# Moving one column in sixteen from VectorE to ScalarE in a streaming variance kernel, with a re-cut tail

## The chip, the cores and the metric

The kernel runs on one core of one Trainium2 chip. The metric is the device time of one execution, in microseconds (us). Engines: ScalarE is ACT, VectorE is DVE, GpSimd is POOL, and SyncE (SP) only issues DMAs here; TensorE does no work.

## The reference

```python
# x: 32 x 512 x 1024, float32
mean_sq = np.mean(x**2, axis=-1)
sq_mean = np.mean(x, axis=-1)**2
return (mean_sq - sq_mean).astype(np.float32)      # 32 x 512
```

It is the variance of each of the 16,384 rows of 1024 numbers. Every row is read once (67.1 MB), and one number a row is written.

## The kernel before

**Columns.** A "column" is 128 rows of 1024 numbers, one row a partition: 128 columns in all, 0.52 MB each. Columns 0 to 95 pass through a loop as six groups of 16, through two buffers `xt[0]` and `xt[1]` of 16 columns. Columns 96 to 127 are the tail, with loads of its own that get smaller: 8, 8, 5, 4, 2, 2, 1 and 1 columns (`END_LOADS`, L51), and the last column in two halves (`PIECES`, L55). The first 16 tail columns land in `xt[0]`, the others in `xt_end`.

**Two ways to a variance.** DVE takes a column with two `bn_stats` of 512 numbers each (L118, or L244 and L248 in the tail, L260 for the last column) and one `bn_aggr` that joins the two halves (L225 in the loop, L253 and L267 in the tail). ACT takes a column with two passes over its 1024 numbers: L122 sums to the negated mean, L127 squares with that mean as bias and sums to the variance. Each ACT pass is followed by an instruction that reads the accumulator. ACT makes several means and then as many variances: a "batch" of three columns in the loop (`ACT_BATCH`).

**A group in the loop.** DVE waits for the landing (L215) and gives ACT the word to begin (`go`, L216). ACT has the first 6 columns of the 16 (`NACT`, L49), DVE the other 10: twenty `bn_stats`, then ten `bn_aggr`. Ahead of the last of these, DVE waits until ACT has finished its 6 columns (`act_done`, L224); the last `bn_aggr` then raises `done` (L226). SP waits on `done` before it loads the next group into the freed buffer (L157, L158); the tail's loads wait for the fifth `done`, which is group 4's (L159), and follow one another on SP (L161 to L169).

**The tail.** `END_WHO` (L52) says who takes which tail column: 11 go to ACT and 20 to DVE, and the last column of all to DVE. DVE can begin the tail only behind the last `bn_aggr` of the last group. For the first 11 of its tail columns (`JOINED`, those in the first two loads) DVE makes the `bn_stats` alone, and POOL joins the halves in nine steps and a last one for each unbroken run of columns (L180 to L209). The other 9, and the last column, DVE joins itself, one column behind.

**Stores.** SP writes columns 0 to 15 early (L306), columns 16 to 120 when POOL, ACT and DVE have passed certain steps (L307 to L310), and the last 7 columns when ACT and DVE are done (L311 to L313).

**Where the code lies.** L146 and L147 place the code of ACT and DVE from slot 128 (`HEAD`) of a block of 256 instruction slots. By the built program, DVE has 128 instructions from that point to the end of the kernel (not counting branches to the very next instruction, which take no time in the trace), and waits that stand by themselves among them.

Of the kernel before, what the change touches and what calls it, by code (L numbers as in the profile page):

```python
# [11 lines left out]
def kernel(  # L12
# [15 lines left out]
    P = nc.NUM_PARTITIONS  # L28
    FP32 = mybir.dt.float32
# [5 lines left out]
    N, D = xf.shape  # L35
    assert N % P == 0
    ncols = N // P
# [6 lines left out]
    GROUP = 16  # L44
    NBUF = 2
    TURNS = 3
    PER_TURN = NBUF * GROUP
    END0 = TURNS * PER_TURN
    NACT = 6  # L49
    ACT_BATCH = 3  # L50
    END_LOADS = [8, 8, 5, 4, 2, 2, 1, 1]  # L51
    END_WHO = "AADDDDDD" "AAADDDDD" "AADDD" "AADD" "DD" "AD" "D" "A"  # L52
    FIRST = END_LOADS[0] + END_LOADS[1]
    JOINED = END_WHO[:FIRST].count("D")
    PIECES = [512, 512]  # L55
    EARLY = 4
    HEAD = 128
# [1 line left out]
    def sbuf(name, shape, dtype):  # L59
        return nc.alloc_sbuf_tensor(name, shape, dtype).ap()  # L60

    def psum(name, shape, dtype):
        return nc.alloc_psum_tensor(name, shape, dtype).ap()

    xt = [sbuf(f"xt{b}", [P, GROUP, D], FP32) for b in range(NBUF)]
    xt_end = sbuf("xt_end", [P, ncols - END0 - FIRST, D], FP32)
    mv = sbuf("mv", [P, 2, ncols], FP32)
    stage = sbuf("stage", [P, PER_TURN, 2], FP32)
    stats = sbuf("stats", [P, PER_TURN, 2, 6], FP32)
    stats_join = sbuf("stats_join", [P, JOINED, 2, 6], FP32)  # L70
    stats_end = sbuf("stats_end", [P, ncols - END0, 4, 6], FP32)
    neg_mean = sbuf("neg_mean", [P, PER_TURN], FP32)
    neg_mean_end = sbuf("neg_mean_end", [P, ncols - END0], FP32)
    two = sbuf("two", [P, JOINED, 2], FP32)
    mu = sbuf("mu", [P, JOINED, 1], FP32)
    dev = sbuf("dev", [P, JOINED, 4], FP32)
    junk = [sbuf(f"junk{i}", [P, D], mybir.dt.bfloat16) for i in range(ACT_BATCH)]
    junk_sq = [psum(f"junk_sq{i}", [P, D], FP32) for i in range(ACT_BATCH)]

    sync, act, dve, gps = nc.sync, nc.scalar, nc.vector, nc.gpsimd  # L80
    landed = [nc.alloc_semaphore(f"landed{b}") for b in range(NBUF)]
    NEND = len(END_LOADS) + len(PIECES)
    landed_end = [nc.alloc_semaphore(f"landed_end{b}") for b in range(NEND)]
# [10 lines left out]
    def load(dst, c0, n, sem, f0=0, f=D):  # L94
        b0, pitch, row0 = next(b for b in BLOCKS if b[0] <= c0 < b[0] + b[1])
        assert c0 + n <= b0 + pitch
        ap = [[pitch * D, P], [D, n], [1, f]] if n > 1 else [[pitch * D, P], [1, f]]
        sync.dma_start(  # L98
            out=dst,
            in_=dataclasses.replace(xf, offset=(row0 + c0 - b0) * D + f0, ap=ap),  # L100
        ).then_inc(sem, 16)
# [10 lines left out]
    def take(engine, sem, n):  # L112
        engine.wait_ge(sem, n)
        engine.sem_inc(sem, -n)  # L114
# [6 lines left out]
    def act_mean(i, xcol, nm):  # L121
        return act.activation(  # L122
            out=junk[i], in_=xcol, func=ACTF.Copy, scale=-S / D, accum_out=nm
        )

    def act_var(i, xcol, nm, var):
        return act.activation(  # L127
            out=junk_sq[i], in_=xcol, func=ACTF.Square, scale=S, bias=nm, accum_out=var
        )

    def end_col(c):
        k = c - END0
        return xt[0][:, k, :] if k < FIRST else xt_end[:, k - FIRST, :]

    end_cols = []
    at = END0
    for b, n in enumerate(END_LOADS):
        end_cols += [(b, c, END_WHO[c - END0]) for c in range(at, at + n)]
        at += n
    assert at == ncols - 1 and sum(PIECES) == D  # L140
    early = END0 + sum(END_LOADS[:EARLY])
    act_step_of, dve_step_of = {}, {}
    joined = [c for b, c, who in end_cols if who == "D"][:JOINED]
    assert joined[-1] < END0 + FIRST and TURNS * NBUF >= NBUF + 1

    for engine in (act, dve):  # L146
        engine.addr_align(FETCH_BLOCK_INSTRUCTIONS, offset=HEAD, max_nops=0)  # L147
# [12 lines left out]
    c = END0  # L160
    for b, n in enumerate(END_LOADS):  # L161
        k = c - END0
# [3 lines left out]
    f = 0  # L166
    for b, n in enumerate(PIECES, len(END_LOADS)):
        load(end_col(c)[:, f : f + n], c, 1, landed_end[b], f, n)
        f += n  # L169

    gps.sem_inc(copied, 1)
    for t in range(TURNS):
# [11 lines left out]
        lambda: gps.tensor_scalar(out=mu, in0=mu, scalar1=0.25, scalar2=None, op0=ALU.mult),  # L184
        lambda: gps.tensor_tensor(out=dev, in0=mean, in1=mu.to_broadcast([P, JOINED, 4]), op=ALU.subtract),
        lambda: gps.tensor_tensor(out=dev, in0=dev, in1=dev, op=ALU.mult),
# [25 lines left out]
    with nc.Fori(0, TURNS, engines=[ENG.DVE]):  # L212
        take(dve, copied, 1)
        for b in range(NBUF):
            take(dve, landed[b], 16)  # L215
            dve.sem_inc(go, 1)  # L216
            mine = range(b * GROUP + NACT, (b + 1) * GROUP)
            for j in mine:
# [11 lines left out]
    for b, c, who in end_cols:  # L230
        if who != "D":
            continue
        if b != seen:
            dve.wait_ge(landed_end[b], 16)
            seen = b
        col = end_col(c)
        if c in joined:
            last = halves(stats_join[:, joined.index(c), :, :], col)
            if c == joined[-1]:
                last.then_inc(dve_step, 1)  # L240
                n += 1
            continue
        st = stats_end[:, c - END0, :2, :]
        dve.bn_stats(out=st[:, 0, :], in_=col[:, :H])  # L244
        if waiting:
            waiting()
        n += 1
        dve.bn_stats(out=st[:, 1, :], in_=col[:, H:]).then_inc(dve_step, 1)  # L248
        dve_step_of.setdefault(b, n)

        def waiting(n=n, c=c, st=st):
            dve.wait_ge(dve_step, n)
            return dve.bn_aggr(out=mv[:, :, c], in_=st)  # L253

    c = ncols - 1
    st = stats_end[:, c - END0, : len(PIECES), :]
    f = 0
    for i, size in enumerate(PIECES):
        dve.wait_ge(landed_end[len(END_LOADS) + i], 16)
        last = dve.bn_stats(out=st[:, i, :], in_=end_col(c)[:, f : f + size])  # L260
        if i == 0:
            waiting()
        f += size
# [7 lines left out]
    with nc.Fori(0, TURNS, engines=[ENG.Activation]):  # L271
        for b in range(NBUF):
            take(act, go, 1)
            for i0 in range(0, NACT, ACT_BATCH):
                mine = range(b * GROUP + i0, b * GROUP + i0 + ACT_BATCH)
                for i, j in enumerate(mine):
                    last = act_mean(i, xt[b][:, i0 + i, :], neg_mean[:, j : j + 1])
                last.then_inc(act_step, 1)
                take(act, act_step, 1)
                for i, j in enumerate(mine):  # L280
                    last = act_var(
                        i, xt[b][:, i0 + i, :], neg_mean[:, j : j + 1], stage[:, j, 1:2]
                    )
            last.then_inc(act_done, 1)
    n = 0
    for b in range(len(END_LOADS)):
        mine = [c for bb, c, who in end_cols if bb == b and who == "A"]
# [59 lines left out]
```

## Time and profile before

| | |
|---|---|
| time, median of 3 runs (lowest, highest) | 163.88 us (163.84, 163.90) |
| time of the profiled execution, and its span | 163.92 us, 162.6 us |
| busy: DVE, ACT, POOL | 103.8, 106.3, 3.6 us |
| HBM read, mean rate over the span | 67.11 MB, 413 GB/s |
| share of the DMA engines' span taken by loads and stores | 96.4% |
| `bn_stats` L118 in the loop | 120, mean 677 ns |
| ACT's mean pass L122, and its accumulator read | 41, mean 1043 ns; 186 ns |
| ACT's variance pass L127 in the loop, and its accumulator read | 36, mean 1104 ns; 186 ns |
| DVE's wait for ACT ahead of the last `bn_aggr` of a group | 0.88 us in each of the six |

The span is what the profiler saw of the program itself; the execution is 1.3 us longer. Durations of neighbouring instructions overlap a little (an engine starts the next before the last has quite ended), so that a run of them is reckoned by the distance between starts, which the timeline gives.

### The profile page before, as it was taken

The numbers are of one execution on the slowest core, as the hardware profiler recorded it, in microseconds if no ns is written. First come the engines' busy times: TensorE is split into PE (matmuls) and PEld (weight loads), VectorE is DVE, ScalarE is ACT, GpSimd is POOL, SyncE is SP. The second block draws the span as 40 slices with busy tenths as digits, with TensorE's granted clock in tenths as the row PEclk, the third lists the DMA queues.
The fourth block names the chain that finished last, engine by engine and source line by source line (L and its number), as shares of the span: only waits on it lengthen the run. The fifth ranks groups of instructions, "written<-read, shape, count | busy, mean of one in ns | idle before, by whom it ended". The sixth has DMA issues, their size and how long they took to land. (4 is left out here: it accounts for less than half of the span.)

```text
span 162.6 us, 570 instructions
## 1 busy us (share of the span) xinstructions
DVE 103.8 (64%) x232; ACT 106.3 (65%) x189; POOL 3.6 (2%) x18
## 2 busy tenths in 40 slices
DVE  0000029980599607994099922998049979999994
ACT  3000029990599807995099932999149999799965
POOL 0000000000000000000000000000000000006000
DMA  7969979989998996996996997997989999999990
GB/s 262 516 290 484 516 322 451 516 355 419 516 419 355 516 484 290 516 500 274 516 500 274 516 516 306 468 516 339 435 387 427 468 395 417 448 416 409 414 356 7
DMA packets 2739, 67.20 MB, mean 413 GB/s; under 512 B 688, under 2 KB 688, under 8 KB 1200
## 3 DMA queue, kind: packets, MB, share of 16 engines
q1 hardware_dynamic: 2736, 67.18, 96.4%
q14 instruction: 3, 0.02, 0.1%
HBM read 67.11 MB, written 0.07 MB: 413 GB/s over the span
## 5 line engine op out<-in xcount | busy, mean ns | idle before, releaser
L118 DVE BATCH_NORM_STATS2 stats<-xt 128x6 f32<-128x512 f32 x120 | 71.8, 677 | 50.0 <-DVEq L114 50.0
L122 ACT ACTIVATE junk<-xt 128x1024 bf16<-128x1024 f32 x41 | 42.7, 1043 | 49.1 <-ACTq L114 48.0
L127 ACT ACTIVATE junk_sq<-xt,neg_mean 128x1024 f32<-128x1024 f32 x36 | 39.7, 1104 | 1.5
L118 DVE BATCH_NORM_STATS2 stats_join<-xt 128x6 f32<-128x512 f32 x22 | 13.2, 676 | 0.0
L225 DVE BATCH_NORM_AGGREGATE stage<-stats 128x2 f32<-128x12 f32 x60 | 6.0, 166 | 6.2 <-DVEq L114 5.3
L122 ACT ACTIVATION_READ_ACCUMULATOR junk<-xt 128x1 f32 x41 | 7.6, 186 | 0.0
L122 ACT ACTIVATE junk<-xt_end 128x1024 bf16<-128x1024 f32 x6 | 6.3, 1046 | 1.4 <-DMA xt_end<-in_x_dram 1.4
L127 ACT ACTIVATE junk_sq<-xt_end,neg_mean_end 128x1024 f32<-128x1024 f32 x6 | 6.7, 1110 | 0.1
L127 ACT ACTIVATION_READ_ACCUMULATOR junk_sq<-xt,neg_mean 128x1 f32 x36 | 6.7, 186 | 0.0
L244 DVE BATCH_NORM_STATS2 stats_end<-xt_end 128x6 f32<-128x512 f32 x9 | 6.1, 678 | 0.4 <-DMA xt_end<-in_x_dram 0.4
L248 DVE BATCH_NORM_STATS2 stats_end<-xt_end 128x6 f32<-128x512 f32 x9 | 5.8, 642 | 0.0
L127 ACT ACTIVATE junk_sq<-xt,neg_mean_end 128x1024 f32<-128x1024 f32 x5 | 5.5, 1105 | 0.1
L174 POOL COPY mv<-stage 128x32 f32<-128x32 f32 x3 | 0.6, 209 | 133.2 <-DVE stage L225 133.2
L270 ACT ACT_TABLE_LOAD x1 | 1.3, 1283 | 2.8 <-PEq L154 2.8
L253 DVE BATCH_NORM_AGGREGATE mv<-stats_end 128x2 f32<-128x12 f32 x9 | 1.7, 192 | 0.0
L260 DVE BATCH_NORM_STATS2 stats_end<-xt_end 128x6 f32<-128x512 f32 x2 | 1.3, 669 | 0.5 <-DMA xt_end<-in_x_dram 0.5
L127 ACT ACTIVATION_READ_ACCUMULATOR junk_sq<-xt_end,neg_mean_end 128x1 f32 x6 | 1.1, 187 | 0.0
L122 ACT ACTIVATION_READ_ACCUMULATOR junk<-xt_end 128x1 f32 x6 | 1.1, 186 | 0.0
L127 ACT ACTIVATION_READ_ACCUMULATOR junk_sq<-xt,neg_mean_end 128x1 f32 x5 | 0.9, 187 | 0.0
L182 POOL TENSOR_TENSOR two<-stats_join 128x22 f32<-128x22 f32 x1 | 0.3, 252 | 12.9 <-DVE stats_join L118 12.9
L201 POOL TENSOR_SCALAR mv<-mu 128x6 f32<-128x6 f32 (+1 forms) x2 | 0.5, 237 | 0.2
L187 POOL TENSOR_SCALAR dev<-dev 128x44 f32<-128x44 f32 x1 | 0.3, 332 | 0.1
(12 smaller groups left out, 2.3 us busy)
## 6 DMA issues: line engine op xcount, KB each, us to landing
xt<-in_x_dram SPq DMA_DIRECT2D x2, 4096.0 KB, 19.5
xt_end<-in_x_dram SPq DMA_DIRECT2D x1, 2560.0 KB, 29.8
xt_end<-in_x_dram SPq DMA_DIRECT2D x1, 2048.0 KB, 34.1
xt_end<-in_x_dram SPq DMA_DIRECT2D x2, 1024.0 KB, 37.2
xt_end<-in_x_dram SPq DMA_DIRECT2D x2, 512.0 KB, 40.4
xt_end<-in_x_dram SPq DMA_DIRECT2D x2, 256.0 KB, 40.9
xt<-in_x_dram SPq DMA_DIRECT2D x6, 24.5
out_dram<-mv SPq DMA_DIRECT2D x1, 52.5 KB, 5.3
```

Of the source, the lines that this page charges most:

```text
L118: last = dve.bn_stats(out=st[:, h, :], in_=xcol[:, h * H : (h + 1) * H])
L122: return act.activation(out=junk[i], in_=xcol, func=ACTF.Copy, scale=-S / D, accum_out=nm)
L127: return act.activation(out=junk_sq[i], in_=xcol, func=ACTF.Square, scale=S, bias=nm, accum_out=var)
L174: gps.tensor_copy(out=mv[:, 1, t * PER_TURN : (t + 1) * PER_TURN], in_=stage[:, :, 1]).then_inc(copied, 1)
L182: lambda: gps.tensor_tensor(out=two, in0=mean[:, :, 0:2], in1=mean[:, :, 2:4], op=ALU.add),
L201: lambda j=j, c=c, n=n: gps.tensor_scalar(out=mv[:, 1, c : c + n], in0=mu[:, j : j + n, 0], scalar1=1.0 / D, scalar2=None, op0=ALU.mult,)
L225: last = dve.bn_aggr(out=stage[:, j, :], in_=stats[:, j, :, :])
L244: dve.bn_stats(out=st[:, 0, :], in_=col[:, :H])
L248: dve.bn_stats(out=st[:, 1, :], in_=col[:, H:]).then_inc(dve_step, 1)
L253: return dve.bn_aggr(out=mv[:, :, c], in_=st)
L260: last = dve.bn_stats(out=st[:, i, :], in_=end_col(c)[:, f : f + size])
L270: act.preload_act_table(ACTF.Square)
```

## The change

ACT takes 7 of the 16 columns of a group, in batches of 4 and 3, and DVE 9. Four scratch buffers of ACT in place of three. The tail's loads become 8, 7, 6, 4, 2, 2, 1, 1 and two halves; of its columns ACT takes 10 and DVE 21 and the last. POOL joins 15 of DVE's tail columns in place of 11: those of the first three loads. The last column moves to the slot of `xt[0]` that the shorter second load leaves free. DVE's code in the loop and tail has 7 instructions fewer: a column's three, twice, in the loop, and one in the tail: 121 in place of 128 by the same count.

```diff
-    NACT = 6
-    ACT_BATCH = 3
-    END_LOADS = [8, 8, 5, 4, 2, 2, 1, 1]
-    END_WHO = "AADDDDDD" "AAADDDDD" "AADDD" "AADD" "DD" "AD" "D" "A"
+    NACT = 7
+    ACT_BATCHES = [(0, 4), (4, 7)]
+    END_LOADS = [8, 7, 6, 4, 2, 2, 1, 1]
+    END_WHO = "ADDDDDDD" "AAADDDD" "AADDDD" "AADD" "DD" "AD" "D" "A"
     FIRST = END_LOADS[0] + END_LOADS[1]
-    JOINED = END_WHO[:FIRST].count("D")
+    JOINED = END_WHO[: FIRST + END_LOADS[2]].count("D")
...
-    xt_end = sbuf("xt_end", [P, ncols - END0 - FIRST, D], FP32)
+    xt_end = sbuf("xt_end", [P, ncols - 1 - END0 - FIRST, D], FP32)
...
-    junk = [sbuf(f"junk{i}", [P, D], mybir.dt.bfloat16) for i in range(ACT_BATCH)]
-    junk_sq = [psum(f"junk_sq{i}", [P, D], FP32) for i in range(ACT_BATCH)]
+    junk = [sbuf(f"junk{i}", [P, D], mybir.dt.bfloat16) for i in range(4)]
+    junk_sq = [psum(f"junk_sq{i}", [P, D], FP32) for i in range(4)]
...
     def end_col(c):
         k = c - END0
+        if c == ncols - 1:
+            return xt[0][:, FIRST, :]
         return xt[0][:, k, :] if k < FIRST else xt_end[:, k - FIRST, :]
...
-            for i0 in range(0, NACT, ACT_BATCH):
-                mine = range(b * GROUP + i0, b * GROUP + i0 + ACT_BATCH)
+            for i0, i1 in ACT_BATCHES:
+                mine = range(b * GROUP + i0, b * GROUP + i1)
```

More of the change, by code (lines that the diff above doesn't have):

```diff
@@ L143 @@
     joined = [c for b, c, who in end_cols if who == "D"][:JOINED]
-    assert joined[-1] < END0 + FIRST and TURNS * NBUF >= NBUF + 1
     for engine in (act, dve):
```

## The prediction

> **What bounds the kernel now.** First the page: its DMA line and queues say that loads move through most of the span.
>
> ```profile
> span 162.6 us, 570 instructions
> ...
> DMA  7969979989998996996996997997989999999990
> ...
> q1 hardware_dynamic: 2736, 67.18, 96.4%
> ```
>
> The dips are no pauses: a load moves in packets of 64 KB, and the engines finish them together. Groups begin on DVE every 19.36 us (61.89, 81.25, 100.61, 119.96), and 8.39 MB in 19.36 us is 433 GB/s, all along. So up to the last landing the loads set the pace. Next, what a group costs behind its landing, from the timeline (start, length, engine):
>
> ```profile
> 81.25 11.96 DVE L118 BATCH_NORM_STATS2 stats<-xt 128x6 f32<-128x512 f32 x20 [5.37 <-DVEq L114]
> 93.36 0.79 DVE L225 BATCH_NORM_AGGREGATE stage<-stats 128x2 f32<-128x12 f32 x9
> 95.03 0.21 DVE L225 BATCH_NORM_AGGREGATE stage<-stats 128x2 f32<-128x12 f32 x1 [0.88 <-DVEq L114]
> ```
>
> DVE's last join of the group stands 0.88 us behind the nine others: it waits for ACT. ACT is the longer engine in every group (all six have this row), and 5.4 us of the period are left for both. Third, the last group and the tail on DVE, and the end:
>
> ```profile
> 133.74 0.21 DVE L225 BATCH_NORM_AGGREGATE stage<-stats 128x2 f32<-128x12 f32 x1 [0.88 <-DVEq L114]
> 133.92 13.15 DVE L118 BATCH_NORM_STATS2 stats_join<-xt 128x6 f32<-128x512 f32 x22
> ...
> 146.99 0.68 DVE L244 BATCH_NORM_STATS2 stats_end<-xt_end 128x6 f32<-128x512 f32 x1
> ...
> 157.44 0.69 DVE L244 BATCH_NORM_STATS2 stats_end<-xt_end 128x6 f32<-128x512 f32 x1 [0.38 <-DMA xt_end<-in_x_dram]
> ...
> 159.31 0.69 DVE L260 BATCH_NORM_STATS2 stats_end<-xt_end 128x6 f32<-128x512 f32 x1 [0.51 <-DMA xt_end<-in_x_dram]
> ...
> 160.71 0.21 DVE L267 BATCH_NORM_AGGREGATE mv<-stats_end 128x2 f32<-128x12 f32 x1
> ```
>
> DVE enters the tail late (the first tail load has landed before 133.5) and works without a break for 23 us; it meets the loads only at 157.44, on its last column but one. Its slack over the whole tail is then small: the waits shown, 0.38 and 0.51 us. The chain that ended last agrees that the end is a landing and one column of ACT:
>
> ```profile
> 117.94 40.75 DMA xt_end<-in_x_dram
> 158.70 0.02 issue
> 158.72 1.16 ACT junk L122 x2
> 159.88 0.02 issue
> 159.90 1.24 ACT junk_sq L127 x2
> ```
>
> ACT ends at 161.15 and DVE at 160.92; the last store is issued at 161.17 and the span ends 1.4 us later.
>
> Last, the DMA queues of the stretch from 155 to 157 us hold one row of another kind:
>
> ```profile
> q14 instruction: 1, 0.01, 1.1%
> ```
>
> It is a fetch of code, 8 KB, at 155.9 us; from 3 to 155 us there is none. At that moment DVE is some 8 instructions ahead of the end of the 128 that the kernel has for it. The landings around it: the one-column load that DVE waits for came at 157.4, where 155.1 for the two columns ahead (ACT starts on them at 155.16) and 0.52 MB at 433 GB/s (1.2 us) gives 156.4. In the packet records fifteen of the sixteen shares of that load are in by 156.15, and one comes at 157.42. So the fetch holds one DMA engine back by about 1.0 us, and all later landings with it.
>
> **The change part by part.**
>
> *ACT's seventh column in the loop.* ACT's means start 1.04 us apart (24.28, 25.32), its variances 1.13 (27.73, 28.86). There are still two batches, so their fixed gaps stay. A group on ACT becomes 2.17 us longer: 13.6 + 2.17 = 15.8 us. In the loop this is covered: the next group lands 19.36 us after this one. DVE's column that goes (two `bn_stats` 0.594 us apart and a join of 0.07) is 1.26 us less, but DVE waits for ACT already: its wait grows from 0.88 to 0.88 + 2.17 + 1.26 = 4.3 us, and the time of `done` goes 2.17 us later. What waits for `done`: SP with the next group's load, POOL's copies (nothing waits long for those), and, behind the wait on DVE itself, the next group (not landed yet) or, after group 5, the whole tail.
>
> *Loads issued 2.17 us later.* Before, the load into the freed buffer is issued at 37.21, 56.56, 75.91, 95.26 and (tail) 114.62, each 5.3 us ahead of the next group's start; now 3.2 us ahead. In the packet records the first of the 16 engines runs out 1.4 us before the group's start (41.15 against 42.55), so 1.8 us are left to begin. Bounds on the start of a load: the last, tiny store needs 0.8 us from its issue to the first packet, 1.0 to the last; the very first load of the program, issued at 0.87 as all engines begin, has its first packet 1.0 and its sixteenth engine 2.06 us later. By the store nothing is lost (margin 0.8 us); by the slowest engine of the first load 2.06 - 1.77 = 0.3 us a group. I take nothing, by the store, which was issued in mid-program; 4 x 0.3 = 1.2 us is the other end (the fifth, the tail's, only moves landings that DVE no longer waits for).
>
> *The tail on DVE.* It starts 2.17 us later: 133.92 + 2.17 = 136.09, ACT's last variance of group 5 being at the same distance ahead of it. Then 15 columns without own joins: 30 x 0.594 = 17.82 (before: 22 of them from 133.92 to 146.99, 0.594 apart), so the first L244 is at 153.91. Then 6 columns joined by DVE, whose pace before was 7.48 us from the first L244 (146.99) to the seventh (154.47): 161.39. The last column takes 1.59 us from first L260 to the end of L267 (160.92 - 159.31, less 0.02 for a start without a wait): 162.98. Does a landing come later than that? No: the loads' bytes are the same in total and nearly so by place (three loads end at column 21 as before, at 145.3 us), and DVE needs each 2 us or more after it landed before (the closest: the last halves, 159.3 against 161.4). So DVE no longer meets the loads at all, and ends at 162.98 against 160.92.
>
> Checked the other way: without its waits DVE would have ended at 159.84 before. Four more joined columns at 1.19 and three fewer own at 1.26 are +0.98, the late start +2.17: 162.99.
>
> *ACT's tail.* It starts 2.17 us later with one column less (2.17 + 0.2 of a batch): about level. Its last column still waits for its landing, so ACT ends at 160.1 to 161.15: no longer last.
>
> *POOL's joins.* They begin at 154.0, when DVE's 15th column is through, and now have three runs: 12 steps at 0.33 (before: 11 from 147.16 to 150.76), a little longer for 15 columns: done by 158.4. The second store then goes out at 158.5 in place of 154.98 and has to be in by 163. Its 52.5 KB find nearly empty queues after 158; the last store needs 1.4 us in all. No cost; if it did queue 5.3 us as before, it would cost 1 us.
>
> *The code fetch.* DVE's code is 7 shorter, so the place that set off the fetch is now reached in the last two instructions, when all loads have landed. The landings of the last three loads come up to 1.0 us earlier. It is worth nothing here, since DVE ends over 3 us behind them.
>
> The Trainium skill, "Runtime: NRT & Kernel Launch", section "Instruction fetch mechanics", says that crossing a block of code costs one bump of a DMA queue and is mostly hidden. By that page this edit is worth nothing anywhere; by the row of this trace up to 1.0 us of landings; in the sum above it is nothing either way.
>
> *Sum.* The end of the last engine moves from ACT's 161.15 to DVE's 162.98: +1.83, and 0.05 for the order of SP's two waits (before, it stood at ACT's; DVE's is waited for first, L312, and ends at 0.02 with 0.04 to the store). 163.92 + 1.88 = **165.8 us**, against a median of 163.88: 1.2% slower.
>
> **The rivals.**
>
> *The loads run dry (slower still).* The start of a load takes the 2.06 us of the program's first load rather than the store's 0.8 to 1.0. For: the margin of 1.8 us is thin. Against: a store in mid-program is quick. 4 x 0.3 = +1.2, as group 5 lands so much later and DVE's chain hangs on it: 167.0. Chance 0.11.
>
> *The end is set by landings (faster).* If DVE kept up, the fetch's 1.0 us would be won: landings at 157.7, ACT done at 160.1, time 162.9. For: the fetch is in the trace, and the tail is cut for it. It decides only if DVE's tail starts by 160.1 - 26.89 = 133.2, that is, if ACT took its seven columns in some 13 us, less than the 13.6 that its six take now. Nothing in the rows makes a pass shorter; a pass's length is the same in all groups. Chance 0.03.
>
> *A slip that costs less than reckoned.* DVE's tail is 3.1 us longer and later, but some of it is returned: the joins' pace with fewer neighbours, or the store path. 164.0 to 165.2; middle 164.7. Chance 0.07, of which 0.02 within 0.2% of before.
>
> *The fetch does not move.* It is then still masked by DVE: same time as the forecast.
>
> **How the numbers follow.** Forecast 0.79 (165.5 to 166.1), dry loads 0.11, cheaper slip 0.07, faster 0.03. The range takes the forecast and the smaller bubbles above it (half of 1.2 us) and a little of the cheaper slip: 165.2 to 166.7. A difference of 0.2% (0.33 us) is about what a measurement of this kernel can tell from none. Slower: 0.79 + 0.11 + 0.05 = 0.95; within 0.2%: 0.02; faster: 0.03.
>
> **What would show it.** In the changed kernel's profile: DVE's wait ahead of its last join of a group at 4.3 us in place of 0.88; groups still 19.36 us apart (more means dry loads); the tail's first `bn_stats` 16.1 us after the last group's start; no wait of DVE for a DMA in the tail; the chain that ended last going through DVE's tail and ACT's group 5 instead of a landing; the instruction queue's packet gone from 155 to 157 us. The prediction is wrong if the last group's `act_done` comes less than 15 us behind its landing, or if DVE waits for a load again.

## The result, and the profile after

The changed kernel takes 168.37 us (median of 6 runs, 167.72 to 169.25) against 163.78 us (6 runs, 163.63 to 163.90) of the kernel before: 1.0279 times as long, 95% interval 1.0248 to 1.0310. The forecast was slower, by 1.9 us; it became 4.6. The execution that was profiled took 167.84 us with a span of 166.1, against 163.92 and 162.6.

The page of the changed kernel, its span, its DMA line and the loads' queue:

```profile
span 166.1 us, 572 instructions
...
DMA  7979996999899699979999999999799999999960
...
q1 hardware_dynamic: 2736, 67.18, 95.3%
```

Beside the page of before, the same bytes fill a little less of a longer span. Where, the timeline of DVE shows (start, length, engine, line):

```profile
81.19 10.78 DVE L118 BATCH_NORM_STATS2 stats<-xt 128x6 f32<-128x512 f32 x18 [3.19 <-DVEq L114]
92.11 0.71 DVE L226 BATCH_NORM_AGGREGATE stage<-stats 128x2 f32<-128x12 f32 x8
97.14 0.21 DVE L226 BATCH_NORM_AGGREGATE stage<-stats 128x2 f32<-128x12 f32 x1 [4.31 <-DVEq L114]
101.87 10.78 DVE L118 BATCH_NORM_STATS2 stats<-xt 128x6 f32<-128x512 f32 x18 [4.52 <-DVEq L114]
...
121.57 10.78 DVE L118 BATCH_NORM_STATS2 stats<-xt 128x6 f32<-128x512 f32 x18 [3.55 <-DVEq L114]
...
137.52 0.21 DVE L226 BATCH_NORM_AGGREGATE stage<-stats 128x2 f32<-128x12 f32 x1 [4.31 <-DVEq L114]
```

DVE's wait for ACT is 4.31 us, as reckoned. But group 4 starts at 101.87 where before it was 100.61, and group 5 at 121.57 against 119.96: 1.6 us late. The busy times by stage, one group a row (stage, its length, DVE, ACT, POOL busy, clock, DMA share, GB/s), before:

```profile
61.89:81.25 19.36, 12.96 (x30) 13.36 (x24) 0.00 (x0) 1.00 1.00 433
81.25:100.61 19.36, 12.96 (x30) 13.35 (x24) 0.21 (x1) 1.00 1.00 433
```

and after:

```profile
61.85:81.19 19.34, 11.70 (x27) 15.52 (x28) 0.00 (x0) 1.00 1.02 430
81.19:101.87 20.68, 11.70 (x28) 15.52 (x28) 0.21 (x1) 1.00 0.97 409
101.87:121.57 19.70, 11.70 (x28) 15.52 (x28) 0.00 (x0) 1.00 0.95 406
```

Neither engine is busy longer in the long groups than in the short one: it is the loads that came late. The chain that ended last (start, length) is now DVE's tail alone, without a landing in it:

```profile
137.52 0.06 DVE stage L226
...
137.71 17.90 DVE stats_join L118 x30
155.61 0.59 DVE stats_end L245
...
163.78 0.56 DVE stats_end L261
164.35 0.02 issue
164.37 0.21 DVE mv L268
```

The profiled execution's 3.92 us more are: group 5 later by 1.61; DVE's tail begun 16.14 us behind it in place of 13.96, and 26.87 long (to 164.58); the end moving from ACT's 161.14 to DVE's, and 0.05 more from there to the last store; and 0.42 us that lie outside the span (167.84 - 166.1 = 1.74; before 1.32). The six runs have 1.71 to 1.75 us outside their spans, so that is not chance; the spans themselves go from 166.0 to 167.5.

### The profile page after: what moved, and what is told of

The parts are those of the page before. It is cut to its first block, busy times and chain, and to the rows that moved or that the text cites. A ratio compares the mean times of both kernels' runs of the same rounds, so it can differ in the third digit from the quotient of the medians.

```text
span 166.1 us, 572 instructions
## 1 busy us (share of the span) xinstructions
DVE 97.0 (58%) x213; ACT 117.3 (71%) x209; POOL 4.0 (2%) x19
## 5 line engine op out<-in xcount | busy, mean ns | idle before, releaser
L118 DVE BATCH_NORM_STATS2 stats<-xt 128x6 f32<-128x512 f32 x108 | 64.7, 677 | 40.8 <-DVEq L114 40.8
L122 ACT ACTIVATE junk<-xt 128x1024 bf16<-128x1024 f32 x46 | 47.9, 1042 | 39.6 <-ACTq L114 38.7
L127 ACT ACTIVATE junk_sq<-xt,neg_mean 128x1024 f32<-128x1024 f32 x42 | 46.3, 1103 | 1.5
L122 ACT ACTIVATION_READ_ACCUMULATOR junk<-xt 128x1 f32 x46 | 8.6, 186 | 0.0
L127 ACT ACTIVATION_READ_ACCUMULATOR junk_sq<-xt,neg_mean 128x1 f32 x42 | 7.8, 186 | 0.0
L118 DVE BATCH_NORM_STATS2 stats_join<-xt_end 128x6 f32<-128x512 f32 x8 | 4.8, 682 | 0.0
L127 ACT ACTIVATE junk_sq<-xt,neg_mean_end 128x1024 f32<-128x1024 f32 x4 | 4.4, 1108 | 0.1
L245 DVE BATCH_NORM_STATS2 stats_end<-xt_end 128x6 f32<-128x512 f32 x6 | 4.1, 681 | 0.0
L249 DVE BATCH_NORM_STATS2 stats_end<-xt_end 128x6 f32<-128x512 f32 x6 | 3.9, 650 | 0.0
L261 DVE BATCH_NORM_STATS2 stats_end<-xt 128x6 f32<-128x512 f32 x2 | 1.3, 660 | 0.0
L202 POOL TENSOR_SCALAR mv<-mu 128x4 f32<-128x4 f32 (+1 forms) x3 | 0.7, 234 | 0.3
```

The costliest lines, as they stand in the source:

```text
L118: last = dve.bn_stats(out=st[:, h, :], in_=xcol[:, h * H : (h + 1) * H])
L122: return act.activation(out=junk[i], in_=xcol, func=ACTF.Copy, scale=-S / D, accum_out=nm)
L127: return act.activation(out=junk_sq[i], in_=xcol, func=ACTF.Square, scale=S, bias=nm, accum_out=var)
L202: lambda j=j, c=c, n=n: gps.tensor_scalar(out=mv[:, 1, c : c + n], in0=mu[:, j : j + n, 0], scalar1=1.0 / D, scalar2=None, op0=ALU.mult,)
```

## The experiments

The "lead" in what follows is the time from the issue of a group's load to the moment when the first of the 16 DMA engines ends the load ahead of it; both are from the trace (issues, packet records). The records don't name a packet's engine, so packets that end and packets that start are paired in order of time. Spans are given to 0.1 us, so a difference between an execution's time and its span is good to 0.05.

**The loop alone, and the tail alone.** The change cut in two. The first kernel has ACT's seven columns and the old tail:

```diff
-    NACT = 6
-    ACT_BATCH = 3
+    NACT = 7
+    ACT_BATCHES = [(0, 4), (4, 7)]
...
```

> Only the loop is changed (ACT 7 of 16 columns); the tail is the one of before. Theory D (dry loads): the load into a freed buffer is issued 2.2 us later, some DMA engines run dry at a hand-over, group 5 begins 1 to 3 us later than 119.96, DVE's tail starts 16.1 us behind that. DVE's end without dry loads would be 159.84 + 2.17 = 162.0, so a time of 164.8, 165.2 if the code fetch goes past the end; with dry loads 166.2 to 168. Theory R (the re-cut tail with its other load sizes makes the loads late): 164.8 to 165.2 and group 5 at 119.96.

Measured: 167.12 us (166.66 to 167.99), 1.0219 times before (1.0186 to 1.0252). In its profile one group takes most of the loss:

```profile
42.59:63.57 20.98, 11.70 (x27) 15.52 (x28) 0.21 (x1) 1.00 1.03 447
63.57:83.08 19.51, 11.70 (x27) 15.52 (x28) 0.00 (x0) 1.00 0.92 383
83.08:102.44 19.36, 11.70 (x28) 15.52 (x28) 0.21 (x1) 1.00 1.01 433
```

and group 5 begins at 121.77. The second kernel has the old loop and the new tail:

```diff
-    END_LOADS = [8, 8, 5, 4, 2, 2, 1, 1]
-    END_WHO = "AADDDDDD" "AAADDDDD" "AADDD" "AADD" "DD" "AD" "D" "A"
+    END_LOADS = [8, 7, 6, 4, 2, 2, 1, 1]
+    END_WHO = "ADDDDDDD" "AAADDDD" "AADDDD" "AADD" "DD" "AD" "D" "A"
...
```

> Only the tail is changed; the loop is the one of before, so loads are issued on time. Theory D: group 5 begins at 119.96, DVE's tail takes 0.98 us more, from 133.92 to 160.8, which the landings set anyway: 163.6 to 164.2. Theory R (the re-cut tail makes the loads late): over 165.

Measured: 163.57 us (163.34 to 163.82), 0.9986 times (0.9976 to 0.9996); group 5 at 119.92. So the late groups are the loop's, and the loop by itself costs 3.3 us of the 4.6. The new tail by itself costs nothing that a measurement can tell. Behind the new loop it does cost, because there DVE's tail ends the kernel: it takes 26.87 us in the changed kernel and 25.90 in the loop-only run, 0.97 more, where 0.98 was reckoned. In the tail-only run the code fetch falls behind the work, at 162.04, and the landings show it: ACT begins the last column at 157.69 in place of 158.72, and ACT's end is no longer last; the chain ends with DVE's tail at 160.76.

**Only ACT's time.** The kernel before, with a seventh pair of passes on ACT whose result goes to a spare place, so that no column moves:

```diff
+    ACT_BATCHES = [(0, 4), (4, 7)]
...
+                    var = stage[:, j, 1:2] if i0 + i < NACT else spare
+                    last = act_var(i, xt[b][:, i0 + i, :], neg_mean[:, j : j + 1], var)
...
```

> The kernel before with one more mean and variance pass on ACT in each group, whose result goes to a spare place: DVE keeps its ten columns and the tail its cut. Only ACT's time per group, and with it the issue of loads and the start of DVE's tail, is later by 2.17 us. Theory D: 164.8 without dry loads, 166 to 168 with them; group 5 begins 1 to 3 us after 119.96. Theory R and any theory that needs the moved columns: 164.8, group 5 at 119.96.

Measured: 166.74 us (166.63 to 168.62), 1.0217 times (1.0158 to 1.0276). The first load into a freed buffer leads by 1.4 us, against 3.9 before; the group behind it takes 20.90 us:

```profile
42.76:63.66 20.90, 12.96 (x30) 15.52 (x28) 0.21 (x1) 1.00 1.03 442
```

Group 5 begins at 121.76. The late issue is enough; the moved columns are not needed.

The same with half the addition, a mean pass alone (1.04 us in place of 2.17):

```diff
...
-                    last = act_var(
-                        i, xt[b][:, i0 + i, :], neg_mean[:, j : j + 1], stage[:, j, 1:2]
-                    )
+                    if i0 + i < NACT:
+                        last = act_var(
+                            i, xt[b][:, i0 + i, :], neg_mean[:, j : j + 1], stage[:, j, 1:2]
+                        )
```

> The kernel before with one more mean pass on ACT in each group (1.04 us, result unused). The loads' lead over the first engine's running dry falls from 3.94 to 2.9 us, against 1.8 with the whole column. Theory D with the start of a load needing under 2.5 us: no loss, group 5 at 119.96, DVE's end 159.84 + 1.04 = 160.9, time 163.8 to 164.0. Rival: any cut of the lead costs in proportion, then half of the 1.8 us that the whole column cost: 164.6 to 165.

Measured: 163.96 us (163.73 to 164.46), 1.0007 times (0.9997 to 1.0017). The median is what comes out if the lead still covers the start of every load, but it does not always: the profiled execution, at 164.46, has groups of 19.73 and 19.83 us with leads of 2.7 to 3.0 us, and group 5 at 120.72, 0.76 late. That execution is the slowest of the ten. So a loss can begin at a lead just under 3 us, and in the median it is far less than half of what the whole pass pair costs: it does not grow in proportion to the time taken from the lead.

**The load issued early.** If the late issue is the cause, the changed kernel must come back when only that is mended. Each group's load is cut in two: DVE's nine columns are loaded anew when DVE has read them, ACT's seven when ACT is through.

```diff
-        sync.wait_ge(done, g - NBUF + 1)
-        load(xt[g % NBUF], g * GROUP, GROUP, landed[g % NBUF])
+        sync.wait_ge(free, g - NBUF + 1)
+        load(xt[g % NBUF][:, NACT:, :], g * GROUP + NACT, GROUP - NACT, landed[g % NBUF])
+        sync.wait_ge(done, g - NBUF + 1)
+        load(xt[g % NBUF][:, :NACT, :], g * GROUP, NACT, landed[g % NBUF])
...
             take(dve, dve_step, 1)
+            dve.sem_inc(free, 1)
...
```

> The changed kernel, each group's load in two parts: DVE's nine columns are loaded anew as soon as DVE has read them (some 4.9 us earlier than the whole), ACT's seven when ACT is through. Theory D (engines run dry because the load is issued too late): groups 19.36 us apart again, group 5 at 119.9 to 120.1, DVE's tail still 16.1 us behind it, DVE's end at 163.0 to 163.2, time 165.8 to 166.3, and runs within 0.3 us of one another. Rival T (seven columns on ACT, or its four buffers, disturb the transfers themselves): 167.5 to 168.5 as without the split, and a spread of 1 us.

Measured: 166.44 us (166.36 to 166.62), 1.0160 times (1.0143 to 1.0177). The groups are even again, and so are the runs:

```profile
62.10:81.53 19.43, 11.69 (x28) 15.52 (x28) 0.00 (x0) 1.00 1.00 432
81.53:100.95 19.42, 11.70 (x27) 15.52 (x28) 0.21 (x1) 1.00 1.00 432
100.95:120.38 19.43, 11.70 (x28) 15.52 (x28) 0.00 (x0) 1.00 1.00 428
```

The two loads cost 0.07 us a group, so that group 5 is at 120.38; DVE's tail starts 16.14 us behind it. It is 0.14 us over the expected range. Most of the 1.9 us that it takes off the changed kernel are the late loads; 0.3 are time outside the span (1.46 us here). The prediction's sum comes out here: 163.92 + 1.88, and 0.42 for group 5 and 0.14 outside the span, are 166.36, as the profiled execution took.

**No wait of DVE for ACT.** DVE's late start into the tail can be taken away too: SP and GpSimd wait for ACT and DVE by themselves, and DVE goes on.

```diff
         sync.wait_ge(done, g - NBUF + 1)
+        sync.wait_ge(act_done, g - NBUF + 1)
...
         gps.wait_ge(done, (t + 1) * NBUF)
+        gps.wait_ge(act_done, (t + 1) * NBUF)
...
             for j in mine:
-                if j == mine[-1]:
-                    take(dve, act_done, 1)
                 last = dve.bn_aggr(out=stage[:, j, :], in_=stats[:, j, :, :])
```

In the changed kernel:

> The changed kernel, DVE no longer waiting for ACT at the end of a group: SP and GpSimd wait for both. Loads are still issued late (lead about 2.1 us, the hop over DVE saved). Theory D with two separate losses: the late start of DVE's tail goes (it starts some 11.7 us behind the last group in place of 16.1), the late landings stay at 1 to 1.6 us, so the end is set by landings and ACT: 164.0 to 165.3. Rival (the late tail is all of the loss, the late landings are a by-product): 163.0 to 163.4.

Measured: 165.35 us (165.00 to 166.32), 1.0106 times (1.0060 to 1.0151), 0.05 over the expected range and far from the rival's. DVE's tail starts 11.6 us behind group 5, but group 5 is late still:

```profile
61.86:82.04 20.18, 11.56 (x27) 15.52 (x28) 0.00 (x0) 1.00 0.96 416
82.04:101.40 19.36, 11.56 (x27) 15.52 (x28) 0.21 (x1) 1.00 1.01 433
101.40:122.39 20.99, 11.56 (x28) 15.52 (x28) 0.00 (x0) 1.00 0.98 415
```

Two losses, then, each with a repair of its own: the tail's start, and the loads. With both repairs in the changed kernel:

> The changed kernel with both repairs: the load in two parts, and no wait of DVE for ACT. Theory D: both losses go; group 5 at 120.0 to 120.4, last landings without the fetch's delay, ACT's last column from 157.9 to 160.3: 163.0 to 163.6, no more than 0.8 us under the kernel before. Rival (something else in the change costs time): over 164.

Measured: 164.28 us (163.72 to 164.71), 1.0029 times (1.0013 to 1.0044): over what was expected, and in the rival's range. In the profiled execution (163.73) all is as reckoned up to the end: group 5 at 120.36, ACT's last column from 158.10, a span of 162.0; 1.73 us lie outside it. Seven of the ten runs took 0.5 to 1.0 us longer than that one, inside their spans (162.5 to 163.0), and there is no trace of them; what they wait for stays open. Each repair takes off less where the other is in place: the split load 1.9 us alone and 1.1 beside the other, the wait taken off DVE 3.0 and 2.2.

And with the tail-only kernel, six columns on ACT:

> The changed tail with the loop of before (six columns on ACT), and DVE no longer waits for ACT at the end of a group: SP and GpSimd wait for both instead. The wait of 0.88 us ahead of DVE's last join goes, so DVE's tail starts at 133.0 in place of 133.88 and DVE ends at 159.9. Theory D and F: landings as in the tail-only run, ACT's end 160.1 sets the end: 162.8 to 163.1. Rival (DVE's tail is not what ends last there): 163.5 as without this.

Measured: 163.24 us (162.95 to 163.45), 0.9959 times (0.9944 to 0.9973): faster than both kernels, and 0.14 over the expected range. DVE's tail starts 1.1 us earlier than before (132.82 in place of 133.92; 0.9 was expected):

```profile
119.93 11.96 DVE L118 BATCH_NORM_STATS2 stats<-xt 128x6 f32<-128x512 f32 x20 [6.39 <-DVEq L114]
132.04 0.86 DVE L227 BATCH_NORM_AGGREGATE stage<-stats 128x2 f32<-128x12 f32 x10
132.82 7.75 DVE L118 BATCH_NORM_STATS2 stats_join<-xt 128x6 f32<-128x512 f32 x13
```

and the end is again a landing with one column of ACT behind it, 1.0 us earlier than in the kernel before:

```profile
117.62 40.05 DMA xt_end<-in_x_dram
157.67 0.02 issue
157.70 1.16 ACT junk L122 x2
158.86 0.02 issue
158.88 1.24 ACT junk_sq L127 x2
```

**Where the code lies.** Four runs shift DVE's code alone. In the changed kernel, seven slots on:

```diff
-    for engine in (act, dve):
-        engine.addr_align(FETCH_BLOCK_INSTRUCTIONS, offset=HEAD, max_nops=0)
+    act.addr_align(FETCH_BLOCK_INSTRUCTIONS, offset=HEAD, max_nops=0)
+    dve.addr_align(FETCH_BLOCK_INSTRUCTIONS, offset=HEAD + 7, max_nops=0)
```

> The changed kernel, DVE's code placed 7 slots further on, so that the code fetch is set off before the kernel's end again. Theory F (the 0.4 us more between span and execution, 1.74 against 1.32, is the fetch that now comes after the end): time less span back to 1.3, the instruction queue's packet back inside the span, median about 0.4 us under the changed kernel's, near 168.0 against 168.4 with the dry loads as they are. Theory G (that 0.4 us is something else): time less span stays at 1.7.

Measured: 168.09 us (167.56 to 169.60), 1.0249 times (1.0232 to 1.0266). The code fetch is back inside the span, at 161.5 us, and the profiled execution (169.60, span 168.3, group 5 as late as 123.76) has 1.3 us outside its span. One slot on (HEAD + 1):

> The changed kernel, DVE's code placed one slot further on, so that its last instruction stands where that of the loop-only run stood. Theory S (the 0.42 us behind the span comes of the very slot at which DVE's code ends: it was there for the changed kernel and for the code-7-earlier run, which end at the same slot, and not for the loop-only run one slot on): time less span 1.3, no code fetch inside the span, time 0.4 us under the changed kernel's as the loads fall: 166.8 to 169. Rival (the seven fewer instructions cost it at any slot): time less span 1.7.

Measured: 168.22 us (167.40 to 168.61), 1.0269 times (1.0227 to 1.0311), the profiled one 167.99 with a span of 166.6: 1.39 outside, with group 5 at 122.10. So one slot is enough to lose the 0.4 us outside the span, and the later loads of these runs hide it in the medians. In the kernel before, seven slots earlier (HEAD - 7):

> The kernel before, DVE's code placed 7 slots earlier, so that the code fetch is set off behind the last landing. Theory F (the fetch holds one DMA engine back by 1.0 us): last landings 1.0 us earlier, DVE begins the last column at 158.3, ACT done at 160.1, time 162.8 to 163.0, or 163.2 to 163.4 if the fetch then costs 0.4 us behind the span. Rival (the fetch is hidden, the late share has another cause): 163.7 to 163.9 with the landings as before.

Measured: 163.72 us (163.58 to 164.01), 0.9994 times (0.9985 to 1.0004): the rival's range, but with earlier landings, which the rival did not have. The fetch did not go behind the end: it came at 26.8 us, in the loop's first turn, in this row of the DMA queues from 20 to 30 us:

```profile
q14 instruction: 1, 0.01, 0.2%
```

There too it held one engine back: the 16 shares of a load (one to each DMA engine) ended 0.8 us apart before it (21.81 to 22.62), 1.06 apart after it (41.14 to 42.20), and so to the end. That is less than the 1.0 us of a fetch in the tail: ACT's last column starts at 158.07, 0.65 earlier than before, and the span is 0.6 shorter (162.0). The 1.68 us outside the span take most of that back. Last, the kernel that was fastest, with DVE's code two slots on (HEAD + 2):

> The kernel that the runs so far point to: the changed tail, the loop of before with six columns on ACT, no wait of DVE for ACT at a group's end, and DVE's code two slots further on, so that it ends at the slot at which the tail-only run's ended (1.29 us between span and execution, 1.71 without the shift). Group 5 at 119.9, DVE's tail from 132.8, ACT's last column from 157.7, span 161.6: 162.9 to 163.3, faster than the kernel before by 0.3 to 0.55%. If the slot is not what the 0.4 us came of here: 163.2 to 163.4.

Measured: 163.92 us (163.62 to 164.07), 1.0006 times (0.9997 to 1.0015), over both ranges. All engines end as without the shift (159.98 and 160.13), but the fetch now falls at 161.19 us, between the issue of the last store (160.16) and its landing. The DMA queues of the last 2.6 us:

```profile
q14 instruction: 1, 0.01, 1.2%
...
out_dram<-mv SPq DMA_DIRECT2D x1, 3.5 KB, 2.4
```

The store takes 2.4 us from issue to landing: fifteen of its sixteen shares are in by 161.56, and one comes at 162.53, with its last packet right behind the fetch. Without the shift the fetch comes at 162.93, behind the store:

```profile
out_dram<-mv SPq DMA_DIRECT2D x1, 3.5 KB, 1.4
```

The span is 1.0 us longer for it, 162.6 against 161.6.

## Why the prediction was wrong

**What held.** Where the loads come on time, the sum stands: in the split-load run DVE's tail starts 16.14 us behind group 5 (16.13 reckoned), in the changed kernel it takes 26.87 us (26.89). DVE's wait for ACT is 4.31 us (4.3). The late start and the longer tail (0.97 us) add as they were added. POOL's joins begin at 155.69 and end by 159.81, and the store behind them, issued at 159.84, lands in 2.0 us: no cost. ACT ends at 162.68, 1.9 us ahead of DVE: not last. DVE waits for no load in its tail, and ACT ends the last group 15.8 us behind its start, so neither of the two signs named for a wrong prediction came; the one that came stands among its checks: groups more than 19.36 us apart.

**The step that failed: "Loads issued 2.17 us later".** It took nothing for it, by the start of the last store, 0.8 to 1.0 us from issue to packets, and gave the loads running dry a chance of 0.11 and a price of 1.2 us. They ran dry in every run of the changed kernel, if the longer spans of those without a trace are read so: it costs 1.6 us in the profiled execution, and over the six runs 1.5 to 3.0 (spans of 166.0 to 167.5 less the 164.5 of the sum). The rival named the right mechanism, but its chance and its price were taken from rows that do not bear on it: a store that finds idle queues (it is issued at 161.17 us, behind the last landing, and not in mid-program, as the prediction has it), and a load at the start of the program. In the middle of a saturated stream the packet records show something else. With a lead of 1.86 us, loads 2 and 3 of the changed kernel began without a gap; load 4, with 1.82, had an engine idle for 0.78 us at least, and its first packets took up to 3.38 us in place of 2.42. In the loop-only run one engine began load 2 at 43.17, 3.7 us after its issue. Since a group has landed only when its slowest engine is through, one late engine is enough. The trace of before had only leads of 3.9 us and could not show where the loss begins; the runs put it between 3.0 and 3.4 us, though not every load with less lead is late:

| lead of an issue (us) | kernel | groups' lengths (us) | group 5 at |
|---|---|---|---|
| 3.9 | before | 19.36 all | 119.96 |
| 3.4 to 3.6 | before, code 7 slots earlier | 19.47, 19.23, 19.47, 19.23 | 120.30 |
| 2.7 to 3.0 | one more mean pass on ACT | 19.36, 19.73, 19.32, 19.83 | 120.72 |
| 1.6 to 2.4 | changed, no wait of DVE | 19.36, 20.18, 19.36, 20.99 | 122.39 |
| 1.8 to 2.1 | changed | 19.36, 19.34, 20.68, 19.70 | 121.57 |
| 1.8, then 0.1 to 1.8 | changed loop, old tail | 20.98, 19.51, 19.36, 19.33 | 121.77 |
| 1.5, then 0.0 to 1.6 | changed, code 7 slots on | 21.14, 19.93, 20.30, 19.61 | 123.76 |
| 1.4, then 0.4 to 1.8 | seventh pass pair on ACT | 20.90, 19.39, 19.35, 19.36 | 121.76 |

In the kernel before with its code earlier the groups take 19.35 us on average, and group 5 is later only by as much as group 1 already was (42.90 in place of 42.55). How late an engine is varies from one execution to the next: the three traces of the changed loop and tail, with the code in three places, have group 5 at 121.57, 122.10 and 123.76. That is the likely reason why the changed kernel's runs spread over 1.5 us and those of the split load over 0.3. What in the start of a load takes up to 3.7 us under load no run here separates. The range failed with it: its upper end, 166.7, took in half of that 1.2.

**A second step, smaller: "The code fetch ... It is worth nothing here".** The fetch is gone from the last loads, as said, and the landings no longer carry it. But the shorter code was not free: some 0.4 us more lie outside the span in all six runs. Shifting DVE's code by one or by seven slots takes it away (1.39 and 1.3 us outside), so the place of the code is the cause. By the count of instructions, DVE's code ends at slot 248 in the changed kernel, in the kernel before shifted by -7, and in the one with both repairs; the profiled executions of those three have 1.68 to 1.74 us outside their spans. At 249 (loop alone, one slot on) it is 1.36 and 1.39, at 254 and 255 1.3. Between them lie cases that this does not order (246: 1.58, 250, the split load: 1.46, 252: 1.71), and the changed kernel's trace records no fetch after the one at 1.9 us, so that no run shows what these 0.4 us are. That part stays open.

**The sum, corrected.** 163.92 + 1.88 + 1.61 (late loads) + 0.42 (outside the span) = 167.83; the profiled execution took 167.84.

The Trainium skill, "Runtime: NRT & Kernel Launch", section "Instruction fetch mechanics", calls the crossing of a block mostly hidden. If the fetches of these traces are such crossings, which no run here shows, the measured rows differ from that, though not in each of them. A fetch put one share 1.0 us behind in the last loads of the kernel before and of the one with the seventh pass pair (159.95 to 161.30 for its last two shares, which were 0.3 apart until then), and 1.0 us in the last store of the shifted kernel. In two others (the mean pass alone, fetch at 157.60, and the code 7 slots on, at 161.52) the last share of a load, 1.1 to 1.2 us behind the first already, came no later.

## What to carry to other kernels

Slack behind a busy transfer queue is not the time until the next landing: with two buffers, ask how long ahead of the running dry of the first DMA engine the next load is issued, and take its price from a load under the same traffic, or leave it open, never from a transfer that met idle queues. An instruction that waits for another engine only to pass the word on holds back everything behind it on its own engine; let the one who needs both events wait for both (here 1.1 us of a tail, and with the new tail the only version that beat the kernel before by more than 0.2%, 163.24 us). Where a few tenths matter, look for the code fetch in the trace and see what transfer it falls upon.

## What the runs showed of the hardware that was not expected

- A 64 KB packet took 2.42 us when it was queued in time. As the first of a load issued less than 3 us ahead it took up to 3.38 us in the changed kernel and up to 3.89 in another run, and engines stood idle for up to 1.4 us besides. The first packets of the program's first load took up to 3.28 us too.
- The loss does not repeat in every group: in the run with the seventh pass pair one group took 20.90 us and the next three 19.35 to 19.39, though their loads were issued only 0.4 to 1.8 us ahead of the first engine's end. A likely reason, not shown, is that the engine that was late is then late in ending too, and so has its next load in time. It is no rule: with the code 7 slots on, each of the four groups was late.
- A code fetch of 8 KB, whose own packet takes 0.3 to 0.6 us once the loop runs, held a DMA engine back by some 0.3 us (among 64 KB packets), 1.0 us (among 4 KB packets), and 1.0 us (across the last store). With one instruction fewer on DVE (the tail-only run) it came 6.1 us later than in the kernel before; which instruction sets it off was not settled.
